# Neighbourhood attention of a two-layer transformer: head pairs scored on the two halves of the rows, position bias added in PSUM, high and low parts of the values side by side in one stationary operand

## The chip, the core and the metric

The kernel runs on one core of a Trainium2 chip. The metric is the device time of one execution in microseconds (us), as the median of several runs. The core has five engines that take their instructions from queues of their own: TensorE (PE in the profile, with its weight loads as PEld), VectorE (DVE), ScalarE (ACT), GpSimd (POOL) and SyncE (SP), which here only issues DMAs.

## The reference

The reference is a two-layer transformer over 256 latent and 256 context tokens, with a width of 1024. Each layer has a feed-forward block, a mixer and another feed-forward block, with adaptive norms between them. The mixer of the second layer is the neighbourhood attention: 16 heads of 64 channels, the 256 latent tokens as a grid of 4 rows by 64 columns, and each query attending to the 16 nearest columns in all 4 rows and to all 256 context tokens.

```
def row_step(args):
    r, q_row = args
    ...
    bias = rpb_cols[:, row_off].transpose(0, 2, 1, 3)
    s_lat = jnp.einsum('bchd,brckhd->bhcrk', q_row, k_nb) * scale + bias
    s_ctx = jnp.einsum('bchd,bkhd->bhck', q_row, k_ctx) * scale
    p = jax.nn.softmax(jnp.concatenate([s_lat.reshape(...), s_ctx], axis=-1), axis=-1)
    ...
    return (jnp.einsum('bhcrk,brckhd->bchd', p_lat, v_nb)
            + jnp.einsum('bhck,bkhd->bchd', p[..., kr * kc:], v_ctx))
```

After it, `y_l = o_l @ w_out` is multiplied by a gate and added to the residual.

## The kernel before

All products run in 32 bits. An operand x is split into a high part of 12 bits and the rest: `split` (L154) takes one ScalarE copy (L156) and one VectorE subtraction (L157). A product of two split operands is then three matmuls, high by high, high by low and low by high (`mm3`, L159 to L162), accumulated in PSUM. So nearly all of the kernel's matmuls stand on lines L160, L161 and L162, and are told apart in the profile by the names of their tiles.

The order of the instructions on each engine is not the order of the text alone: the framework's scheduler lays the operations of independent pieces between each other and sets the queues' order when the kernel is built. On the chip each engine then keeps that order, and waits at an instruction whose inputs are not there. Tiles come from pools of a fixed number of buffers: `pu` has 4 banks of PSUM, `pd` and `ps` have 2 each, `wp` holds 3 raw weight pieces and 4 split ones, `tp` (tiles named by `T`) has 10 buffers, `gp` (`G`) 10.

The neighbourhood attention is `mixer_c` (L931). It works in four steps of four heads (`half`, L940), that is two chunks of 128 channels, each with two heads `m` on partitions 0 to 63 and 64 to 127. A step has these parts:

- The projections of q (256 latent tokens), k and v (512 tokens each), out of weight pieces of 1 MB that SyncE loads (L501) and that are split. q and k come transposed: channels on partitions, tokens along the free axis.
- `scores` (L969), for one head: the position bias is fetched by two DMAs (L982), a mask is added by GpSimd (L983), and the sum is split into `bh` and `bl`. For each of two tiles of 128 queries, three matmuls on the 64 partitions of the head give 512 scores (tiles `k,q`, L991), and two matmuls with the permutation matrix `J` (L992, L993) add the two parts of the bias to the first 256 of them, since the bias comes with its columns reversed. Then VectorE takes the maximum (L662), ScalarE the exponential with its sum (L664), VectorE the reciprocal (L665), and ScalarE scales (L995).
- `values` (L999), for one head: eight transposes of the probabilities (`cst,e`, L672) into two PSUM tiles, each split into `ah` and `al`, and for each of four key tiles the three matmuls of `mm3`: v high by `ah`, v high by `al`, v low by `ah`. The stationary operand is 128 channels wide, that is two heads, and only the 64 rows of the result that belong to the head are read. They are split into `z` (L1007).

The scores of the next head are written ahead of the values of a head (L1014); in the last step three heads are scored ahead. After the fourth step come three parts of the output projection (L1017 to L1019), and then the norm and the last feed-forward block.

The differential attention of the first layer has scores of the same size. There the two halves of a head pair alternate matmul by matmul (L744 to L748):

```
for i in range(3):
    for m in range(2):
        pr = slice(64 * m, 64 * m + 64)
        nc.tensor.matmul(pss[m][:, :n], (qh, qh, ql)[i][pr, qs], (kh, kl, kh)[i][pr, TOK - n :], ...)
```

## Time and profile before

| | |
|---|---|
| median of 3 runs | 1934.93 us (1932.49 to 1937.55) |
| span of the profiled execution, first to last instruction | 1931.2 us |
| PE, PEld busy | 97%, 82% of the span |
| DVE, ACT, POOL busy | 65%, 38%, 4% |
| projections, attention and output projection of the second mixer | from 1490 to 1717 us of the span |

The profile is of one execution. No time of its own besides the span is given for that execution; the span is 3.7 us below the median of the runs. A group's row in the profile gives line, engine and operation, the tiles written and read, the shape, the count, then the busy time in us and the mean duration of one in ns, and behind the second bar the idle time of the engine ahead of these instructions and what ended it. A matmul's duration contains its way through the array, on which the next one already runs; the time that a matmul costs TensorE is the distance from its start to the next start.

### The profile page before, as it was taken

The page shows a single profiled execution, that of the slowest core. Times are in us where ns is not written, and L with a number is a line of the kernel's source. Part 1 is how long each engine was busy: PE and PEld are TensorE (multiplying, and loading weights), DVE is VectorE, ACT ScalarE, POOL GpSimd, SP SyncE. Part 2 cuts the span into 40 slices and gives each one's busy share as a digit, 9 for nine tenths or more (in the row PEclk, how much of TensorE's full clock was granted, in tenths as well). Part 3 has the DMA queues.
Part 4 walks back from the last instruction along what each step waited for, and adds up shares of the span by engine and source line. Part 5 has one row for each costly group of instructions (what it writes and reads, how often), then busy time and mean ns, then how long its engine had stood idle before and what let it go on. Part 6 is the DMA issues. An engine that isn't in the chain of part 4 may idle for free.

```text
span 1931.2 us, 26004 instructions
## 1 busy us (share of the span) xinstructions
PE 1880.6 (97%) x10486; PEld 1586.8 (82%) x10486; DVE 1253.9 (65%) x1948; ACT 740.3 (38%) x1199; POOL 72.3 (4%) x63
## 2 busy tenths in 40 slices
PE   7999999999999999999999999999999999989998
PEld 3878788889877788888888888878889888889998
DVE  5557686666666785976775467763445654576665
ACT  4533233224556234232233242321233555554443
POOL 1000000000100001000000200000000000120000
PEclk9999999999999999999999999999999999989999
DMA  7674555451332322654464224642232333325552
GB/s 260 216 243 171 190 181 196 134 191 30 113 120 77 120 82 80 236 196 153 144 218 161 88 77 163 207 154 84 89 119 84 96 82 80 67 91 193 196 169 73
DMA packets 191153, 271.73 MB, mean 141 GB/s; under 512 B 19703, under 2 KB 139898, under 8 KB 191032
## 3 DMA queue, kind: packets, MB, share of 16 engines
q1 hardware_dynamic: 189468, 267.69, 42.5%
q10 hardware_dynamic: 1260, 2.14, 0.3%
q8 instruction: 82, 1.34, 0.3%
q14 instruction: 39, 0.32, 0.0%
q0 software_dynamic: 304, 0.24, 0.0%
HBM read 262.69 MB, written 7.34 MB: 140 GB/s over the span
## 4 chain that ended last, share of the span: by engine, by line
PE 57%; issue 11%; DVE 3%; DMA 2%; ACT 1%; POOL 1%; SPq 0%; POOLq 0%; DVEq 0%; ACTq 0%
PE pu L160 10%; PE pu L161 10%; PE pu L162 10%; PE pd L160 6%; PE pd L162 6%; PE pd L161 6%; PE ps L160 2%; PE ps L162 2%; PE ps L161 2%; DMA bias<-in_na_rpb_dram 2%; PE ps L672 1%; DVE wl L157 1%; DVE acc L444 1%; PE ps L298 1%; ACT wh L156 0%
## 5 line engine op out<-in xcount | busy, mean ns | idle before, releaser
L162 PE MATMUL pu<-h,wl 128*128 128x512 f32 (+1 forms) x1600 | 544.8, 341 | 3.0 <-POOL wl L157 3.0
L160 PE MATMUL pu<-h,wh 128*128 128x512 f32 (+1 forms) x1600 | 544.4, 342 | 1.8 <-ACT h L488 1.5
L161 PE MATMUL pu<-h,wh 128*128 128x512 f32 (+1 forms) x1600 | 545.4, 341 | 0.1
L156 ACT ACTIVATE wh<-raw 128x1024 fp32r<-128x1024 f32 x228 | 240.6, 1059 | 544.8 <-PE pu L161 417.2
L157 DVE TENSOR_TENSOR wl<-raw,wh 128x1024 fp32r<-128x1024 f32 x216 | 263.0, 1222 | 179.6 <-ACT wh L156 175.3
L160 PEld LDWEIGHTS pu<-h,wh 128*128 128x128 f32 x1600 | 303.1, 190 | 44.5 <-issue 4.2
L162 PEld LDWEIGHTS pu<-h,wl 128*128 128x128 f32 x1600 | 304.0, 190 | 38.5 <-POOL wl L157 3.2
L161 PEld LDWEIGHTS pu<-h,wh 128*128 128x128 f32 x1600 | 304.3, 190 | 34.2 <-DVE h L489 0.7
L287 DVE SCALAR_TENSOR_TENSOR mv<-mw,sF,mv 128x1024 f32<-128x1024 f32 x210 | 258.5, 1279 | 20.9 <-DMA mw<-in_mod_w_dram 20.8
L156 ACT ACTIVATE w<-raw 128x1024 fp32r<-128x1024 f32 x88 | 91.5, 1056 | 163.1 <-PE ps L161 123.4
L552 DVE TENSOR_TENSOR sg<-sg,pu 128x512 f32<-128x512 f32 (+1 forms) x87 | 52.2, 603 | 134.7 <-PE pu L162 127.1
L515 DVE SCALAR_TENSOR_TENSOR res<-pd,gate,res 128x256 f32<-128x256 f32 x244 | 110.9, 478 | 39.8 <-PE pd L162 39.3
L157 DVE TENSOR_TENSOR w<-raw,w 128x1024 fp32r<-128x1024 f32 x88 | 106.9, 1220 | 41.5 <-ACT w L156 41.5
L160 PE MATMUL pd<-g,w 128*128 128x512 f32 (+1 forms) x376 | 133.2, 354 | 0.0
L162 PE MATMUL pd<-g,w 128*128 128x512 f32 (+1 forms) x376 | 132.4, 352 | 0.0
L161 PE MATMUL pd<-g,w 128*128 128x512 f32 (+1 forms) x376 | 132.2, 352 | 0.0
L160 PE MATMUL ps<-g,w 128*128 128x512 f32 (+1 forms) x320 | 116.2, 363 | 0.0
L162 PE MATMUL ps<-g,w 128*128 128x512 f32 (+1 forms) x320 | 116.0, 363 | 0.0
L161 PE MATMUL ps<-g,w 128*128 128x512 f32 (+1 forms) x320 | 116.0, 363 | 0.0
L162 PE MATMUL pd<-h,wl 128*128 128x512 f32 (+1 forms) x288 | 108.2, 376 | 1.6 <-DVE wl L157 1.6
L160 PE MATMUL pd<-h,wh 128*128 128x512 f32 (+1 forms) x288 | 108.6, 377 | 0.0
L161 PE MATMUL pd<-h,wh 128*128 128x512 f32 (+1 forms) x288 | 107.5, 373 | 0.0
(261 smaller groups left out, 2808.6 us busy)
## 6 DMA issues: line engine op xcount, KB each, us to landing
raw<-in_ffn_w_dram SPq DMA_DIRECT2D x132, 1024.0 KB, 5.4
mw<-in_mod_w_dram SPq DMA_DIRECT2D x144, 512.0 KB, 5.9
raw<-in_ab_w_in_dram SPq DMA_DIRECT2D x12, 1024.0 KB, 6.8
raw<-in_na_w_in_dram SPq DMA_DIRECT2D x12, 1024.0 KB
raw<-in_ab_w_out_dram SPq DMA_DIRECT2D x4, 1024.0 KB
raw<-in_na_w_out_dram SPq DMA_DIRECT2D x4, 1024.0 KB
bias<-in_na_rpb_dram SPq DMA_DIRECT2D x32, 96.0 KB, 6.1
dftr<-const_dft_dram SPq DMA_DIRECT2D x5, 256.0 KB
```

The lines of the kernel that those rows point to most:

```text
L156: S.activation(hi, src, AF.Copy)
L157: eng.tensor_tensor(lo, src, hi.bitcast(F32), op=ALU.subtract)
L160: nc.tensor.matmul(ps, wh, xh, start=start, stop=False)
L161: nc.tensor.matmul(ps, wh, xl, start=False, stop=False)
L162: nc.tensor.matmul(ps, wl, xh, start=False, stop=stop)
L287: V.scalar_tensor_tensor(acc, mw, c, acc, op0=ALU.mult, op1=ALU.add)
L298: nc.tensor.matmul(ps[32 * j : 32 * j + 32], row[:, 31 - b : 63 - b], mod_acc[l, i][j % 2][:, j // 2], start=b == 0, stop=b == len(batch) ...
L444: V.tensor_tensor(acc, acc, q, op=ALU.add)
L515: V.scalar_tensor_tensor(res[d][:, sl], ps[:, po], g[:, d, s : s + 1], res[d][:, sl], op0=ALU.mult, op1=ALU.add)
L552: V.tensor_tensor(sg[:, sl], sg[:, sl], p3[:, sl], op=ALU.mult)
L672: nc.tensor.transpose(at[kt // 2][:, o : o + P], e[:, P * kt : P * kt + P], ident)
```

## The change

All of it is in `mixer_c`, and in the constant `J`, which goes.

- The queries are written in reversed columns when they leave PSUM (`turned`). The scores then stand in the order of the fetched bias, and the permutation by `J`, its load and the split of the bias go. VectorE adds the masked bias to the first 256 scores in PSUM.
- `scores` works on two heads. The six matmuls of a query tile alternate between the lower and the upper 64 partitions and write two PSUM tiles. The probabilities of both heads stand in one tile of the pool `gp`.
- The values are stored by head, the 64 high columns beside the 64 low ones. With this stationary operand two matmuls for a key tile, on `ah` and on `al`, give the high products in 64 rows and the low ones in the other 64. ScalarE copies the half of the other rows to the own partitions (`zx`), VectorE adds the two and writes the columns back in their order (`zu`), and the sum is split once for both heads. The product of the low values and `al`, which was left out, is now in the sum.
- The order of the text: per step, scores of the first pair, projection of v, scores of the second pair, values of the first pair, projection of the next q, values of the second pair, projection of the next k. In the last step the first part of the output projection takes the place of the next q.

```diff
-        jt = T(name="jt")[:, :P]
-        nc.sync.dma_start(jt, a["tmp"][:, :P])
-        J = const.tile([P, P], F32R, name="J")
-        S.activation(J, jt, AF.Copy)
...
+        def turned(x):
+            return x.rearrange("p (r c) -> p r c", r=4)[:, :, ::-1]
...
-                S.activation(u, ps[:, :LAT], AF.Copy, scale=0.125)
-                split(*q[i], u)
+                S.activation(turned(u), ps[:, :LAT].rearrange("p (r c) -> p r c", r=4), AF.Copy, scale=0.125)
+                split(*qs[half][i], u)
...
-                split(bh, bl, bias)
...
-                    mm3(ps, q[i][0][pr, qsl], q[i][1][pr, qsl], k[i][0][pr], k[i][1][pr], True, False)
-                    nc.tensor.matmul(ps[:, :256], J, bh[:, e0 : e0 + 256], start=False, stop=False)
-                    nc.tensor.matmul(ps[:, :256], J, bl[:, e0 : e0 + 256], start=False, stop=True)
-                    e, st = softmax_exp(ps, TOK)
-                    S.activation(e, e, AF.Copy, scale=st[:, 2:3])
+                pss = [PU(), PU()]
+                for x, y, n in ((qh, kh, 0), (qh, kl, 1), (ql, kh, 2)):
+                    for m in range(2):
+                        pr = slice(64 * m, 64 * m + 64)
+                        nc.tensor.matmul(pss[m], x[pr, qsl], y[pr], start=n == 0, stop=n == 2)
+                pe = gp.tile([P, 2, TOK], F32, tag="g", name="e")
+                for m in range(2):
+                    ps = pss[m]
+                    V.tensor_tensor(ps[:, :256], ps[:, :256], bias[m][:, e0 : e0 + 256], op=ALU.add)
+                    st = sp.tile([P, 4], F32, tag="sm", bufs=8, name="smx")
+                    V.tensor_reduce(st[:, 0:1], ps, axis=AX.X, op=ALU.max, negate=True)
+                    S.activation(pe[:, m], ps, AF.Exp, bias=st[:, 0:1], accum_out=st[:, 1:2])
+                    V.reciprocal(st[:, 2:3], st[:, 1:2])
+                    S.activation(pe[:, m], pe[:, m], AF.Copy, scale=st[:, 2:3])
...
-                weighted(po, at, 4, lambda kt: [vt[kt // 2][:, kt % 2, x, hs] for x in range(2)])
-                split(zt[pr, i, 0], zt[pr, i, 1], po[pr, :LAT])
+                    w = vt[kt // 2][:, kt % 2, 2 * i + m].rearrange("p a c -> p (a c)")
+                    for n, x in enumerate((ah, al)):
+                        nc.tensor.matmul(po[:, LAT * m : LAT * m + LAT], w, x[:, sl], start=kt == 0 and n == 0, stop=kt == 3 and n == 1)
...
+                S.activation(x[own], po[other, sl], AF.Copy)
+                V.tensor_tensor(turned(u[own]), po[own, sl].rearrange("p (r c) -> p r c", r=4),
+                                x[own].rearrange("p (r c) -> p r c", r=4), op=ALU.add)
+            split(*z[2 * half + i], u)
...
+        for half in range(4):
+            es[half, 0] = scores(half, 0)
+            project_vs(half)
+            es[half, 1] = scores(half, 1)
+            values(half, 0, es[half, 0])
+            if half < 3:
+                project(win, 256 * half + 256, 2, h, project_q(half + 1), PD, [0])
+            else:
+                out_project(wout, range(0, 4), z[0:4], gate, [0])
+            values(half, 1, es[half, 1])
+            if half < 3:
+                project(win, 1024 + 256 * half + 256, 2, h, project_k(half + 1), PD)
```

The change moves instructions on the engines. On TensorE, this is the place before at which the first two heads begin, behind the projection of v (`pd` from `vh,h`): three score matmuls (`k,q`) of one head, then the two of the bias.

```order
L162 MATMUL pd<-vh,h 128x256
L160 MATMUL pu<-k,q 128x512
L161 MATMUL pu<-k,q 128x512
L162 MATMUL pu<-k,q 128x512
L992 MATMUL pu<-bh,J 128x256
L993 MATMUL pu<-bl,J 128x256
L160 MATMUL pu<-k,q 128x512
```

And this is TensorE now at the beginning of the third step, where the projection of k ends and that of v begins; L982 of the changed kernel is the score matmul, L155 to L157 are the three of `mm3`.

```order
L155 MATMUL pd<-h,wh 128x512
L156 MATMUL pd<-h,wh 128x512
L157 MATMUL pd<-h,wl 128x512
L982 MATMUL pu<-k,q 128x512 x12
L155 MATMUL pd<-vh,h 128x256
L156 MATMUL pd<-vl,h 128x256
L157 MATMUL pd<-vh,h 128x256
```

The twelve score matmuls of a pair of heads now stand in one piece, with no bias matmul between them and none behind. Only the very first pair is cut, into two and ten.

On ScalarE, this is the softmax of one head before, in the third step: `e` is the exponential (L664) and its scaling (L995), `ah` the copy of transposed probabilities (L156) of the head ahead of it.

```order
L156 ACTIVATE wh_14026<-raw_14024 128x1024
L156 ACTIVATE z_13249<-pu_13324 64x256
L156 ACTIVATE bh_13348<-bias_13347 128x384
L664 ACTIVATE e_13363,smx_13361<-pu_13355,smx_13361 128x512
L664 ACTIVATE e_13375,smx_13373<-pu_13367,smx_13373 128x512
L995 ACTIVATE e_13363<-e_13363,smx_13361 128x512
L995 ACTIVATE e_13375<-e_13375,smx_13373 128x512
L156 ACTIVATE ah_13390<-ps_13379 128x512
```

And this is ScalarE now in the third step, from the softmax of the second pair (L989, L991) on; the `ah` (L151) belong to the values of the first pair, and `vh` to the weights of the next projection of v.

```order
L989 ACTIVATE e_13237,smx_13239<-pu_13229,smx_13239 128x512
L989 ACTIVATE e_13237,smx_13245<-pu_13230,smx_13245 128x512
L991 ACTIVATE e_13237<-e_13237,smx_13239 128x512
L151 ACTIVATE ah_13282<-ps_13272 128x512
L991 ACTIVATE e_13237<-e_13237,smx_13245 128x512
L989 ACTIVATE e_13258,smx_13260<-pu_13250,smx_13260 128x512
L989 ACTIVATE e_13258,smx_13266<-pu_13251,smx_13266 128x512
L151 ACTIVATE ah_13290<-ps_13273 128x512
L991 ACTIVATE e_13258<-e_13258,smx_13260 128x512
L991 ACTIVATE e_13258<-e_13258,smx_13266 128x512
L151 ACTIVATE ah_13308<-ps_13298 128x512
L151 ACTIVATE vh_13583<-raw_13581 128x1024
```

Two exponentials and a scaling of the second pair now stand ahead of the first `ah` of the first pair, and the rest of that softmax between the next ones. At the same place on TensorE, twelve score matmuls, eight transposes and fourteen matmuls of the next q stand ahead of the first value matmul. On SyncE the eight bias loads of a step now stand in one piece, with three to five weight loads between two such pieces; before they mostly stood in twos and fours between the weight loads. The rest of the program, up to the second mixer and behind it, keeps its order.

More of the change, by code (lines that the diff above doesn't have):

```diff
@@ L51, in constants @@
     cst[:, _CO["ident"]] = np.eye(P)
-    J = np.zeros((P, P))
-    for r2 in range(2):
-        for c in range(64):
-            J[64 * r2 + 63 - c, 64 * r2 + c] = 1.0
-    tmp = np.zeros((P, 384), f32)
-    tmp[:, :P] = J
+    tmp = np.zeros((P, 256), f32)
     cst[:, _CO["sel"]] = np.tile(np.eye(32)[:, :8], (4, 1))
@@ L98 @@
 class _K:
+    pass
 @with_exitstack
@@ L176, in tile_dit @@
     nc.sync.dma_start(w0[:33, :64], a["hy_f_w0"][0])
-    nc.sync.dma_start(w0[:33, 192:448], a["tmp"][:33, P:])
+    nc.sync.dma_start(w0[:33, 192:448], a["tmp"][:33])
     nc.sync.dma_start(w0[:64, 64:192].rearrange("p (i f) -> p i f", i=2), a["hy_f_w1"][0].rearrange("i p f -> p i f"))
@@ new lines, in position, with scores @@
+        def position(hd):
+            b = T(name="bias")[:, :384]
+            b3 = b.rearrange("p (e c) -> p e c", e=6)
+            for r2 in range(2):
+                src = bass.AP(tensor=rpb.tensor, offset=hd * 465 + (5 - r2) * 31 - 48, ap=[[1, 64], [31, 6], [1, 64]])
+                nc.sync.dma_start(b3[64 * r2 : 64 * r2 + 64], src)
+            nc.gpsimd.tensor_tensor(b3, b3, mask, op=ALU.add)
+            return b
+        def scores(half, i):
+            bias = [position(4 * half + 2 * i + m) for m in range(2)]
+            es = []
+            (qh, ql), (kh, kl) = qs[half][i], ks[half][i]
+            for qt in range(2):
+                qsl = slice(P * qt, P * qt + P)
+                e0 = 64 * (2 - 2 * qt)
+                pss = [PU(), PU()]
[12 more added lines that the diff above has]
+                    S.activation(pe[:, m], pe[:, m], AF.Copy, scale=st[:, 2:3])
+                es.append(pe)
+            return es
@@ L1001, in values @@
+        def values(half, i, es):
+            vt = vs[half]
+            po = PU()
+            for m in range(2):
                 at = [PS() for _ in range(2)]
                 for qt in range(2):
-                    transposed(at, es[qt], 4, qt)
-                po = PU()
-                hs = slice(P * i, P * i + P)
-                weighted(po, at, 4, lambda kt: [vt[kt // 2][:, kt % 2, x, hs] for x in range(2)])
-                split(zt[pr, i, 0], zt[pr, i, 1], po[pr, :LAT])
-            heads = [(i, m) for i in range(2) for m in range(2)]
@@ L1010, in mixer_c @@
-            ahead = 1 if half < 3 else 3
-            es = [scores(*hd) for hd in heads[:ahead]]
-            for n, hd in enumerate(heads):
-                if n + ahead < 4:
-                    es.append(scores(*heads[n + ahead]))
-                values(*hd, es[n])
-        gate = gates(1, 5, False)
-        out_project(wout, range(0, 4), z[0:4], gate, [0])
+                    transposed(at, es[qt][:, m], 4, qt)
+                for kt in range(4):
+                    if kt % 2 == 0:
+                        ah, al = T(F32R, name="ah"), T(F32R, name="al")
+                        split(ah, al, at[kt // 2])
+                    sl = slice(256 * (kt % 2), 256 * (kt % 2) + 256)
+                    w = vt[kt // 2][:, kt % 2, 2 * i + m].rearrange("p a c -> p (a c)")
+                    for n, x in enumerate((ah, al)):
+                        nc.tensor.matmul(po[:, LAT * m : LAT * m + LAT], w, x[:, sl], start=kt == 0 and n == 0, stop=kt == 3 and n == 1)
```

70 lines of the change are left out of this document (26 added, 44 removed).

## The prediction

> **What bounds the kernel now.** I first read the page's busy times, then the chain of waits for the pace of the attention's steps, then the busy times of two whole steps.
>
> ```profile
> PE 1880.6 (97%) x10486; PEld 1586.8 (82%) x10486; DVE 1253.9 (65%) x1948; ACT 740.3 (38%) x1199; POOL 72.3 (4%) x63
> ```
>
> ```profile
> 1544.73 1.02 PE ps L672 x8
> ...
> 1594.15 1.02 PE ps L672 x8
> ...
> 1644.72 1.02 PE ps L672 x8
> ```
>
> ```profile
> 1544.73:1594.15 49.42, 47.84 (x313) 41.28 (x314) 25.96 (x46) 27.61 (x56) 3.80 (x5) 1.00 0.35 81
> 1594.15:1644.72 50.57, 49.18 (x313) 42.76 (x314) 25.98 (x46) 27.59 (x56) 3.33 (x4) 0.97 0.33 79
> ```
>
> The same eight transposes return after 49.42 and 50.57 us: one step of four heads takes about 50. The second fence gives, for these two stretches, their length and the busy times of PE, PEld, DVE, ACT and POOL, then the granted clock. In a step PE is busy for 48 to 49 us, DVE for 26, ACT for 27.6. TensorE sets the pace, so a matmul's distance to the next start is worth its full length there, and work on the others is free as long as TensorE does not come to wait for it.
>
> These are the distances, from the order in time on TensorE: six scores of one head and the two matmuls of a projection behind them.
>
> ```profile
> 1524.32 0.50 PE L160 MATMUL pu<-k,q 64*128 64x512 f32 x1
> 1524.66 0.39 PE L161 MATMUL pu<-k,q 64*128 64x512 f32 x1
> 1524.89 0.39 PE L162 MATMUL pu<-k,q 64*128 64x512 f32 x1
> ...
> 1525.90 0.38 PE L160 MATMUL pd<-h,wh 128*128 128x256 f32 x1
> ...
> 1574.35 0.28 PE L161 MATMUL pd<-h,wh 128*128 128x256 f32 x1
> 1574.47 0.28 PE L162 MATMUL pd<-h,wl 128*128 128x256 f32 x1
> ```
>
> A matmul of 512 columns costs 0.23 us, one of 256 columns 0.12. Six scores cost 1.58 us (1524.32 to 1525.90): the first and the step back to 128 rows cost a little more.
>
> **The change part by part.**
>
> *Scores in pairs.* The first layer's attention already alternates the halves, with matmuls of the same shape.
>
> ```profile
> 514.14 1.65 PE L747 MATMUL pu<-qk 64*128 64x512 f32 x12
> 515.73 0.50 PE L160 MATMUL pd<-h,wh 128*128 128x512 f32 x1
> ```
>
> Twelve take 1.59 us there, which twelve at 0.23 could not: the two halves run at the same time. Before, 16 heads cost 16 x 1.58 = 25.3 us; after, 8 pairs cost 8 x 1.59 = 12.7. That is -12.6.
>
> *No `J`.* 16 heads x 4 matmuls of 256 columns, 64 x 0.12 = -7.7 us. Their waits go too:
>
> ```profile
> L992 PE MATMUL pu<-bh,J 128*128 128x256 f32 x24 | 5.9, 323 | 3.0 <-ACT bh L156 3.0
> L992 PE MATMUL pu<-bhl,J 128*128 128x256 f32 x8 | 2.3, 345 | 1.0 <-ACT bhl L156 1.0
> L993 PE MATMUL pu<-bhl,J 128*128 128x256 f32 x8 | 2.0, 306 | 0.2 <-DVE bhl L157 0.2
> ```
>
> TensorE stood idle for 3.0 + 1.0 + 0.2 = 4.2 us ahead of these: -4.2. The bias now has to be there one operation later on VectorE, and its loads stand ahead of the weight loads on SyncE.
>
> ```profile
> L982 SPq DMA_DIRECT2D bias<-in_na_rpb_dram x32: 595/614/646, 1467.1 to 1677.4; - x32
> ...
> DMA to landing us min/median/max: 5.9/6.1/7.4
> ```
>
> The loads of a step, eight of 6 us each and 0.6 us of issue, are asked for when the buffers of the values are free; that is in the values of a step's pairs, some 10 us ahead of the next scores (the last 37 projection matmuls of k alone are 37 x 0.23 = 8.5 us). I take the bias at nothing; if that cover fails, each step waits some us at its first addition. The three weight loads queued behind these are wanted half a step later.
>
> *Values.* 16 heads x 4 key tiles x one matmul of 256 columns less: 64 x 0.12 = -7.7 us.
>
> *Scores no longer laid between values.* Before, six times (two heads in each of the first three steps) the scores of one head were cut up among the values of another, as in this stretch and the next:
>
> ```profile
> 1540.74 0.31 PE L160 MATMUL pu<-ah,v 128*128 128x256 f32 x1
> 1540.98 0.49 PE L160 MATMUL pu<-k,q 64*128 64x512 f32 x1
> ...
> 1544.66 1.09 PE L672 MATMUL ps<-cst,e 128*128 128x128 f32 x8
> 1545.51 0.47 PE L160 MATMUL pd<-h,wh 128*128 128x512 f32 x1
> ```
>
> ```profile
> 1553.08 0.38 PE L160 MATMUL pu<-ah,v 128*128 128x256 f32 x1
> ...
> 1556.78 0.49 PE L672 MATMUL ps<-cst,e 128*128 128x128 f32 x3
> ```
>
> They take 3.92 and 3.70 us, where six scores in one piece and twelve values are 1.58 + 12 x 0.12 = 3.02: each change between 64 and 128 rows costs about 0.1 us. Three of each are 3 x 0.90 + 3 x 0.68 = 4.7; now the values lie only between matmuls of 128 rows: -4.7.
>
> So TensorE is relieved by 12.6 + 7.7 + 4.2 + 7.7 + 4.7 = 36.9 us, 9.2 for each step.
>
> *The new chain of the softmax.* The bias addition in PSUM has no row before. It lies between nothing (the maximum had to read PSUM anyway) and a whole 512-column pass (0.69); nearest is a VectorE operation of its size out of PSUM.
>
> ```profile
> L157 DVE TENSOR_TENSOR v<-pd,v 128x256 fp32r<-128x256 f32 x16 | 6.7, 418 | 3.0 <-ACT v L156 3.0
> L662 DVE TENSOR_REDUCE smx<-pu 128x1 f32<-128x512 f32 x32 | 20.7, 686 | 19.1 <-PE pu L993 18.8
> L156 ACT ACTIVATE ah<-ps 128x512 fp32r<-128x512 f32 x32 | 18.5, 597 | 0.6 <-PE ps L672 0.6
> L157 DVE TENSOR_TENSOR bl<-bias,bh 128x384 fp32r<-128x384 f32 x11 | 6.1, 556 | 9.5 <-ACT bh L156 9.1
> ```
>
> I take 0.42. For a step VectorE then loses 4 splits of `bl` (0.56) and 4 of z (0.42) and gains 8 additions, 4 `zu` and 2 z (0.42 each): 26.0 - 3.9 + 5.9 = 28 us. ScalarE loses 4 `bh` and gains about one operation: below 27. The reversed writes of `u` and `zu` have no row either; even at twice the time they are 24 operations, 10 us of VectorE and ScalarE over the mixer, off the chain except for the very last z, which has some 25 matmuls of the output projection (3 us) ahead of its use. By their sums, neither engine limits a step of 50 - 9.2 = 41 us. Their order does.
>
> The place is the first value matmul of each step. It waits for `ah`, and on ScalarE two exponentials and a scaling of the second pair stand ahead of that.
>
> ```profile
> 1577.96 0.69 ACT L664 ACTIVATE e<-pu,smx 128x512 f32<-128x512 f32 x1 [1.80 <-DVE smx L662]
> ...
> 1578.64 0.68 ACT L664 ACTIVATE e<-pu,smx 128x512 f32<-128x512 f32 x1
> ...
> 1579.30 1.33 ACT L995 ACTIVATE e<-e,smx 128x512 f32<-128x512 f32 x2
> 1580.53 0.38 ACT L948 ACTIVATE u<-pd 128x256 f32<-128x256 f32 x1
> ```
>
> An exponential takes 0.67, a scaling 0.62. From the start of the second pair's scores: its first two tiles are done after half of 1.59 and the rest of a matmul, about 0.95; two additions and a maximum, 2.48; two exponentials, 3.82; a scaling, 4.44; `ah`, 5.04. TensorE has 1.59 of scores, eight transposes (1544.66 to 1545.51, 0.85) and 14 x 0.12 = 1.68 ahead: 4.12. So it waits 0.9 us. The next `ah` and `al` of the pair stand behind the rest of that softmax and the splits of two weights; followed in the same way they come between 0.0 and 0.2 late, five or six times. I take 2.0 us for a step, +8. The ends are 0 (an `ah` with nothing ahead of it on ScalarE would be done at 1.59 + 0.85 + 0.60 = 3.04, before TensorE asks for it) and 4.5 (five such waits, all as long as the first).
>
> *The clock.* In the second stretch above the clock was 0.97, in the first 1.00, and both held one wait of this size:
>
> ```profile
> 1576.21 0.51 PE L992 MATMUL pu<-bh,J 128*128 128x256 f32 x2 [1.34 <-ACT bh L156]
> ...
> 1625.45 0.79 PE L992 MATMUL pu<-bh,J 128*128 128x256 f32 x2 [1.15 <-ACT bh L156]
> ```
>
> One wait of about 1.2 us in two brought 50.57 x 0.03 = 1.5 us of loss. Before there was one such loss among the steps, and I leave one. The Trainium skill (TensorE: Matmul & The Clock Gate, Part 1: The HAM clock gate) has the clock halved only after an idle window of about 3.4 us; by that the new waits would cost no clock at all and my sum would stand, while by the row it could be 1.5 us for each step more. The row speaks against the rule, so the upper end carries it.
>
> *Sum.* -36.9 + 8 = -28.9 us. The span is 1931.2, so 1902.3; what lies around it doesn't change, and from the median of the runs, 1934.93, it is 1906.0 us.
>
> **The rivals.**
>
> *The pairs gain and the evacuation takes it back.* Each pair hands VectorE and ScalarE four tiles at once, and both queues serve them ahead of the next `ah`. For it speaks the 0.9 us above; against it the busy sums, 28 and 27 of 41 us. If the whole gain of the pairing (12.6) is waited for again, it gives 1906 + 12.6 = 1919, and with a clock loss in each step 1925. The Trainium skill (TensorEngine Tiling (Array Packing), Performance Considerations) has the rule: packing speeds up TensorE but not the emptying of PSUM, which may become the bottleneck. 12 in 100.
>
> *The pairs do not run side by side here.* Then the scores cost 96 x 0.23 + 8 x 0.2 = 23.7 instead of 12.7, and it comes to 1917. Against it stands the same form at 514.14. 3 in 100.
>
> *Slower: ScalarE's queue holds the values up.* Between the third and the fourth `ah` stands a copy of the next v weights, which waits for a DMA; were that, or the bias ahead of it on SyncE, late in each step, all values behind would wait. It decides from 9.2 us a step on, where the relief is used up. At 10 us a step and a clock loss each, 4 x 11.5 - 36.9 = +9: 1944. Against it: those loads are asked for most of a step ahead, and the bias needs only 6 to 7 us. 5 in 100.
>
> **How the numbers follow.** The forecast, with new waits of 0 to 4.5 us a step, has 80 in 100: from 1934.93 - 36.9 = 1898 to 1898 + 18 = 1916, and 1896 if the one clock loss goes as well. The rivals have 12, 3 and 5. The range that holds 8 in 10 runs from 1896 to 1921: it takes in the forecast's own range and the first rival up to its middle. A measurement here can tell about 0.3% (5.8 us) from no change. Slower by that needs over 10.7 us of new waits a step: 5 in 100. Within it, 7.8 to 10.7 us a step: 5 in 100. Faster: 90.
>
> **What would show it right or wrong.** Twelve scores from one block to the next in 1.6 us; no idle time at an addition of the bias; a distance between two steps' transposes of 42 to 43 us; idle time of TensorE at the first value matmul of a step of about 1 us and not more than 2 a step in all. It is wrong if steps take 46 us or more, or if the waits stand at bias additions, or if DVE or ACT is busy for over 90% of a step.

## The result and the profile after

| | before | after |
|---|---|---|
| median of the runs on one chip | 1936.24 us (1932.49 to 1938.17) | 1903.98 us (1901.99 to 1906.16) |
| span of the profiled execution | 1931.2 us | 1900.3 us |
| PE, DVE, ACT busy in the span | 1880.6, 1253.9, 740.3 us | 1850.6, 1257.0, 738.0 us |

The ratio is 0.983 (0.982 to 0.985): 32 us less. The prediction said 1906.0 and 1896 to 1921. Its time lies 2 us from the median; its gain, 28.9 us, is 3.4 smaller than the measured 32.3, and not every term of its sum held.

Line numbers are now those of the changed kernel: the matmuls of `mm3` are L155 to L157, `split` L151 and L152, the scores L982, the bias addition L986, the exponential L989, the scaling L991, the transposes L667, the values L1012. The first fence has the busy times of two whole steps, from the first pair's scores to the first pair's scores of the next step (length, then PE, PEld, DVE, ACT, POOL, then the granted clock).

```profile
1552.59:1594.79 42.20, 40.54 (x281) 35.77 (x281) 26.80 (x52) 26.56 (x55) 4.09 (x5) 1.00 0.36 94
1594.79:1636.82 42.03, 41.06 (x282) 35.85 (x282) 26.70 (x52) 26.55 (x55) 4.25 (x5) 1.00 0.35 95
```

A step takes 42.1 us where it took 49.42 and 50.57. For the whole mixer, these are the stretches from its first matmul to the first matmul of the next block, before and after:

```profile
1490.53:1728.18 237.65, 224.19 (x1513) 197.96 (x1513) 140.75 (x262) 132.49 (x267) 25.08 (x21) 0.98 0.33 84
```

```profile
1491.15:1695.61 204.46, 193.09 (x1386) 173.41 (x1384) 141.36 (x285) 128.47 (x258) 23.84 (x18) 0.98 0.33 93
```

The mixer is 33.2 us shorter and the rest of the span 2.3 longer. TensorE's busy time in the mixer fell by 31.1 us, its idle time from 13.5 to 11.4: nearly all of the gain is work that TensorE no longer does. TensorE still sets the pace, and VectorE and ScalarE are busy for 64% of a step. The order in time on TensorE around the second pair of a step (the last bracket of a row is the idle time ahead of it and what ended it):

```profile
1565.89 1.65 PE L982 MATMUL pu<-k,q 64*128 64x512 f32 x12
1567.47 1.09 PE L667 MATMUL ps<-cst,e 128*128 128x128 f32 x8
1569.51 0.39 PE L155 MATMUL pd<-h,wh 128*128 128x256 f32 x1 [0.95 <-ACT e L989]
...
1579.59 0.38 PE L1012 MATMUL pu<-ah,v 128*128 128x256 f32 x1 [0.28 <-ACT ah L151]
1580.41 0.50 PE L155 MATMUL pd<-h,wh 128*128 128x512 f32 x1 [0.43 <-ACT u L943]
```

Twelve scores take 1.58 us from block to block, as in the first layer. Five of the eight pairs run in such a block; the very first is cut into two and ten, and the second pairs of the last two steps take 2.27 and 2.29 us, held up in the middle by a wait for `v`. Over the whole mixer these groups of TensorE wait (behind the second bar: the idle time and its releasers), and VectorE's additions of the bias stand below them:

```profile
L155 PE MATMUL pd<-h,wh 128*128 128x256 f32 (+1 forms) x96 | 33.1, 345 | 1.9 <-ACT e L989 0.9 <-ACT u L943 0.9
L1012 PE MATMUL pu<-ah,v 128*128 128x256 f32 x64 | 19.8, 313 | 1.0 <-ACT ah L151 1.0
L1012 PE MATMUL pu<-al,v 128*128 128x256 f32 x64 | 17.7, 299 | 1.1 <-DVE al L152 1.1
L982 PE MATMUL pu<-k,q 64*128 64x512 f32 x96 | 14.3, 415 | 0.6 <-DVE v L152 0.6
L155 PE MATMUL pd<-vh,h 128*128 128x256 f32 x128 | 36.8, 288 | 0.6 <-DVE v L152 0.6
L155 PE MATMUL pd<-z,wh 128*128 128x256 f32 x64 | 19.0, 297 | 3.0 <-DVE res L510 3.0
L986 DVE TENSOR_TENSOR pu<-pu,bias 128x256 f32<-128x256 f32 x32 | 12.5, 422 | 1.2 <-PE pu L982 1.1
```

The first five add up to 5.2 us of waits in the steps, 1.3 a step. The additions take 0.422 us each and wait for their scores, never for the bias.

### The profile page after: what moved, and what is told of

Read it like the earlier page. It is cut to its first block, busy times and chain, and to the rows that moved or that the text cites. A ratio compares the mean times of both kernels' runs of the same rounds, so it can differ in the third digit from the quotient of the medians.

```text
span 1900.3 us, 25792 instructions
## 1 busy us (share of the span) xinstructions
PE 1850.6 (97%) x10358; PEld 1566.0 (82%) x10358; DVE 1257.0 (66%) x1972; ACT 738.0 (39%) x1190; POOL 73.6 (4%) x63
## 4 chain that ended last, share of the span: by engine, by line
PE 67%; DVE 4%; ACT 2%; issue 1%; POOL 1%; DMA 0%; SPq 0%; DVEq 0%; ACTq 0%
PE pu L155 11%; PE pu L156 11%; PE pu L157 11%; PE pd L155 7%; PE pd L157 7%; PE pd L156 7%; PE ps L155 3%; PE ps L156 3%; PE ps L157 3%; PE pu L1012 1%; DVE wl L152 1%; PE ps L667 1%; DVE acc L439 1%; PE pu L982 1%; PE ps L293 1%
## 5 line engine op out<-in xcount | busy, mean ns | idle before, releaser
L157 PE MATMUL pu<-h,wl 128*128 128x512 f32 (+1 forms) x1600 | 545.6, 342 | 3.0 <-POOL wl L152 3.0
L155 PE MATMUL pu<-h,wh 128*128 128x512 f32 (+1 forms) x1600 | 545.0, 342 | 1.6 <-ACT h L483 1.5
L156 PE MATMUL pu<-h,wh 128*128 128x512 f32 (+1 forms) x1600 | 546.0, 342 | 0.1
L151 ACT ACTIVATE wh<-raw 128x1024 fp32r<-128x1024 f32 x228 | 240.3, 1058 | 558.6 <-PE pu L156 403.2
L152 DVE TENSOR_TENSOR wl<-raw,wh 128x1024 fp32r<-128x1024 f32 x216 | 263.7, 1225 | 203.8 <-ACT wh L151 177.6
L155 PEld LDWEIGHTS pu<-h,wh 128*128 128x128 f32 x1600 | 303.8, 191 | 44.1 <-issue 4.2
L157 PEld LDWEIGHTS pu<-h,wl 128*128 128x128 f32 x1600 | 304.7, 191 | 38.4 <-POOL wl L152 3.3
L156 PEld LDWEIGHTS pu<-h,wh 128*128 128x128 f32 x1600 | 304.9, 191 | 33.8 <-DVE h L484 0.5
L151 ACT ACTIVATE w<-raw 128x1024 fp32r<-128x1024 f32 x88 | 91.5, 1057 | 164.2 <-PE ps L156 120.5
L152 DVE TENSOR_TENSOR w<-raw,w 128x1024 fp32r<-128x1024 f32 x88 | 107.0, 1221 | 42.0 <-ACT w L151 41.9
L155 PE MATMUL pd<-g,w 128*128 128x512 f32 (+1 forms) x376 | 133.6, 355 | 0.0
L157 PE MATMUL pd<-g,w 128*128 128x512 f32 (+1 forms) x376 | 132.6, 353 | 0.0
L156 PE MATMUL pd<-g,w 128*128 128x512 f32 (+1 forms) x376 | 132.6, 353 | 0.0
L155 PE MATMUL ps<-g,w 128*128 128x512 f32 (+1 forms) x320 | 116.3, 363 | 0.0
L157 PE MATMUL ps<-g,w 128*128 128x512 f32 (+1 forms) x320 | 116.1, 363 | 0.0
L156 PE MATMUL ps<-g,w 128*128 128x512 f32 (+1 forms) x320 | 116.1, 363 | 0.0
L155 PE MATMUL pd<-h,wh 128*128 128x512 f32 (+1 forms) x288 | 108.3, 376 | 1.9 <-ACT e L989 0.9
L157 PE MATMUL pd<-h,wl 128*128 128x512 f32 (+1 forms) x288 | 107.6, 374 | 1.7 <-DVE wl L152 1.7
L156 PE MATMUL pd<-h,wh 128*128 128x512 f32 (+1 forms) x288 | 106.9, 371 | 0.0
```

Of the source, the lines that this page charges most:

```text
L151: S.activation(hi, src, AF.Copy)
L152: eng.tensor_tensor(lo, src, hi.bitcast(F32), op=ALU.subtract)
L155: nc.tensor.matmul(ps, wh, xh, start=start, stop=False)
L156: nc.tensor.matmul(ps, wh, xl, start=False, stop=False)
L157: nc.tensor.matmul(ps, wl, xh, start=False, stop=stop)
```

## The experiments

All times are medians of several runs beside runs of the kernel before on the same chip; the ratio to those is given with its interval. Code is shown against the changed kernel.

**The changed kernel a second time.**

> The changed kernel once more, on the same chip as the next three, as what they are measured against. Both theories: 1904 us, that is 32 us below the kernel before (ratio 0.983).

Measured: 1904.4 us, ratio 0.984 (0.982 to 0.985). Its steps repeat those of the first profile (the next one takes 42.04 us):

```profile
1555.31:1597.51 42.20, 40.54 (x281) 35.75 (x280) 26.80 (x52) 26.57 (x55) 3.69 (x4) 1.00 0.37 94
```

So a step's length tells kernels apart to about 0.1 us, while medians of the whole differ by 0.4 us and spans of the same kernel by 2.7 (1900.3 and 1903.0). The experiments are read by their steps first.

**Heads in turn.** The six matmuls of a query tile in the order of the heads, three and three.

```diff
-                for x, y, n in ((qh, kh, 0), (qh, kl, 1), (ql, kh, 2)):
-                    for m in range(2):
+                for m in range(2):
+                    for x, y, n in ((qh, kh, 0), (qh, kl, 1), (ql, kh, 2)):
```

> The same twelve score matmuls of a pair, but the three of the lower half first and then the three of the upper, so that neighbours use the same rows of the array. Theory (TensorE's own time sets the steps): twelve take 2.8 to 3.0 us instead of 1.6, 8 x 1.2 to 1.4 = 10 to 11 us slower than the changed kernel, 1914 to 1915. Rival (the gain is the new order of the projections, and what the pairing saves is waited for again behind the softmax): the first head's scores are there as early as before, TensorE waits less at the values, and the time stays within 2 us of 1904.

Measured: 1903.0 us, ratio 0.983 (0.981 to 0.985). The theory fell, and with it the idea that this edit undoes the pairing; the time that the rival gave was met, but not for the rival's reason. The queue was built as written, three of one PSUM tile and then three of the other:

```
L982 MATMUL pu_12581<-k_12507,q_12377 128x512 x3
L982 MATMUL pu_12582<-k_12507,q_12377 128x512 x3
L982 MATMUL pu_12602<-k_12507,q_12377 128x512 x3
L982 MATMUL pu_12603<-k_12507,q_12377 128x512 x3
```

and yet the trace's order in time has the block last 1.59 us:

```profile
1552.02 1.66 PE L982 MATMUL pu<-k,q 64*128 64x512 f32 x12
1553.61 0.39 PE L155 MATMUL pd<-vh,h 128*128 128x256 f32 x1
```

The halves ran side by side although the queue does not alternate: a matmul on the other half starts while earlier ones of the first half are still waiting. The edit also moved the second pair's scores ahead in the built order, and its steps are shorter than those of the change:

```profile
1552.02:1593.17 41.15, 40.56 (x281) 35.80 (x281) 27.44 (x52) 26.55 (x55) 3.23 (x4) 1.00 0.39 96
1593.17:1634.59 41.42, 40.57 (x281) 35.82 (x281) 27.75 (x52) 26.56 (x55) 4.45 (x4) 1.00 0.36 97
```

**Six and six.** All six matmuls of the lower half (both query tiles), then all six of the upper.

```diff
-            for qt in range(2):
...
+            for m in range(2):
+                pss = [PU(), PU()]
+                for qt in range(2):
...
+                    for x, y, n in ((qh, kh, 0), (qh, kl, 1), (ql, kh, 2)):
+                        nc.tensor.matmul(pss[qt], x[pr, qsl], y[pr], start=n == 0, stop=n == 2)
```

> Both heads of a pair are scored, but first all six matmuls of the lower half (both query tiles), then all six of the upper half. In the run with three and three in turn the halves still ran side by side: the trace has the third matmul of either head start within 0.01 us of each other. Theory: TensorE only looks a few matmuls ahead for work on the other half, so six in a row are too many; the twelve then take 12 x 0.23 + 0.2 = 2.96 us in place of 1.58, 8 x 1.38 = 11 us more for TensorE, of which the waits give back up to two thirds as they did when the third value matmul was put back: 1908 to 1915. Rival: it looks ahead far enough, the twelve take 1.6 us and the time stays from 1901 to 1906.

Measured: 1906.65 us, ratio 0.985 (0.983 to 0.986). The block's length lies between those of the theory and the rival:

```profile
1556.07 2.22 PE L982 MATMUL pu<-k,q 64*128 64x512 f32 x12
1558.22 0.38 PE L155 MATMUL pd<-vh,h 128*128 128x256 f32 x1
```

The block takes 2.15 us, neither 1.58 nor the 2.96 of twelve in a row. That is 0.57 or two and a half slots of 0.23 more than side by side. By the start times of the single matmuls, the first of the upper half begins together with the third of the lower (1556.64), when two are through and four still to do. So the reach here is about four matmuls.

**Apart, and the control side by side.** To keep the halves apart, a matmul of 32 columns over all 128 rows (zeros, overwritten by the scores) stands ahead of each head; the control has the same matmuls ahead of both heads and alternates.

```diff
+        zero = const.tile([P, 32], F32R, name="zero")
+        S.activation(zero, ident[:, :32], AF.Copy, scale=0.0)
...
-                for x, y, n in ((qh, kh, 0), (qh, kl, 1), (ql, kh, 2)):
-                    for m in range(2):
+                for m in range(2):
+                    nc.tensor.matmul(pss[m][:32, :32], zero, zero, start=True, stop=True)
+                    for x, y, n in ((qh, kh, 0), (qh, kl, 1), (ql, kh, 2)):
```

> The two heads of a pair are scored in turn, three matmuls and three, and ahead of each three stands a matmul of 32 columns over all 128 rows (zeros, into the PSUM tile that is overwritten next), so that the halves cannot run side by side: in 12 of the 16 query tiles, since in four the extra matmuls were built far ahead of the scores. The extra matmuls are priced by the run with the same ones ahead of both heads. Theory of the prediction: the pairing is worth its matmuls; a tile apart costs 6 x 0.23 and two more steps to and from 128 rows where side by side it is 3 x 0.23 and one, so 0.95 us more, 12 tiles 11.4 us, of which the waits give back no more than they did for the values (a third): 7 to 12 us above the run side by side, 1912 to 1919. Rival (what the pairs gain is waited for again): within 3 us of the run side by side.

> The changed kernel with the same 32 extra matmuls of 32 columns over 128 rows, both ahead of the alternating six of a query tile, so that the halves still run side by side. It prices what the extra matmuls cost by themselves: 32 at about 0.05 and 16 steps to and from 128 rows at 0.2, 4 to 5 us at most, part of it in waits that are there anyway: 1904 to 1909.

Measured: apart 1920.54 us, ratio 0.992 (0.991 to 0.993); side by side 1906.15 us, ratio 0.985 (0.983 to 0.986). The difference is 14.4 us. Apart:

```profile
1525.32 0.18 PE L983 MATMUL pu<-zero 128*32 128x32 f32 x1
1525.43 0.94 PE L986 MATMUL pu<-k,q 64*128 64x512 f32 x3
1526.30 0.20 PE L983 MATMUL pu<-zero 128*32 128x32 f32 x1
1526.43 0.96 PE L986 MATMUL pu<-k,q 64*128 64x512 f32 x3
```

and side by side:

```profile
1551.45 0.21 PE L983 MATMUL pu<-zero 128*32 128x32 f32 x2
1551.59 0.98 PE L987 MATMUL pu<-k,q 64*128 64x512 f32 x6
1552.50 0.23 PE L983 MATMUL pu<-zero 128*32 128x32 f32 x2
```

One head alone takes 1.0 us (1525.43 to 1526.43), two side by side 1.05 (1551.45 to 1552.50): a tile apart costs 0.95 us more. By the start times 14 of the 16 tiles were apart, two more than expected, so the work is 13.3 us. But the difference is not that work alone. In the profiled executions the mixer, up to the first matmul of the next block, takes 221.3 us apart and 205.9 side by side, 15.4 more. With the heads apart TensorE's clock is at 0.50 twice among the scores, from 1528.97 and from 1607.47, for 3.41 us each; the control has no such loss there, and it makes up 3.4 of the 15.4. And in whole steps a part of the work goes into idle time. Here is a step with three tiles apart, and a step of the control:

```profile
1559.90:1603.85 43.95, 43.95 (x288) 37.52 (x287) 27.36 (x52) 27.09 (x55) 4.31 (x4) 1.00 0.35 90
```

```profile
1551.59:1594.22 42.63, 41.56 (x291) 36.18 (x288) 26.83 (x52) 26.52 (x55) 5.58 (x6) 1.00 0.37 95
```

TensorE is busy for 2.4 us more, its 1.1 us of idle time are gone, and the step is 1.3 longer. So without the clock the pairing is worth some 12 us here: most of its work, as the theory has it, though the difference of the medians lies above the theory's 7 to 12. The rival that the pairs' gain is waited for again, with 3 us at most, has fallen. The scheduler laid out the two queues differently in other places too, so 12 is not exact.

**Values with three matmuls.** The low values in a stationary operand of their own, as before.

```diff
-                    w = vt[kt // 2][:, kt % 2, 2 * i + m].rearrange("p a c -> p (a c)")
-                    for n, x in enumerate((ah, al)):
-                        nc.tensor.matmul(po[:, LAT * m : LAT * m + LAT], w, x[:, sl], ...)
+                    vh, vl = [vt[kt // 2][:, kt % 2, y, P * i : P * i + P] for y in range(2)]
+                    mm3(po[:, LAT * m : LAT * m + LAT], vh, vl, ah[:, sl], al[:, sl], kt == 0, kt == 3)
...
-                S.activation(x[own], po[other, sl], AF.Copy)
-                V.tensor_tensor(turned(u[own]), ...)
+                S.activation(turned(u[own]), po[own, sl].rearrange("p (r c) -> p r c", r=4), AF.Copy)
```

> Values as in the kernel before: the high and the low parts in two stationary operands of 128 channels, three matmuls for a key tile, and no copy of the other half (the low values times al are left out again). The rest as in the changed kernel. Theory: 64 more matmuls of 256 columns, 64 x 0.12 = +7.7 us, 1911 to 1912. Rival (they go into the waits for ah and al that TensorE has there): less than half of it, 1904 to 1907.

Measured: 1906.86 us, ratio 0.985 (0.984 to 0.987). Two steps:

```profile
1552.73:1595.77 43.04, 42.58 (x297) 37.54 (x296) 25.07 (x48) 26.47 (x55) 2.16 (x3) 1.00 0.33 90
1595.77:1638.74 42.97, 42.56 (x297) 37.52 (x297) 25.50 (x48) 26.47 (x55) 3.69 (x5) 1.00 0.34 93
```

TensorE has 1.8 us more to do in a step (42.57 and 40.80, the means), but the step is only 0.9 longer (43.0 and 42.1): its idle time falls from 1.3 us to 0.4. The 16 matmuls of a step cost what they should, and half of that was standing idle anyway. (The edit also takes VectorE's addition of the halves off the way to `z`, which may have shortened a wait.) The groups say the same: of the waits for `ah`, `al`, `e` and `u`, 4.0 us in the changed kernel, 0.8 are left.

```profile
L155 PE MATMUL pd<-h,wh 128*128 128x256 f32 (+1 forms) x96 | 33.0, 344 | 0.2
L155 PE MATMUL pu<-ah,v 128*128 128x256 f32 x64 | 19.7, 308 | 0.5 <-ACT ah L151 0.3
L156 PE MATMUL pu<-al,v 128*128 128x256 f32 x64 | 19.0, 297 | 0.1
```

**The bias by `J` again.** The bias is split and added by the two matmuls with the permutation, here behind the six scores of a query tile; the halves still alternate, and the reversed writes go.

```diff
-                        nc.tensor.matmul(pss[m], x[pr, qsl], y[pr], start=n == 0, stop=n == 2)
+                        nc.tensor.matmul(pss[m], x[pr, qsl], y[pr], start=n == 0, stop=False)
+                for m in range(2):
+                    for n in range(2):
+                        nc.tensor.matmul(pss[m][:, :256], J, bias[m][n][:, e0 : e0 + 256], start=False, stop=n == 1)
...
-                    V.tensor_tensor(ps[:, :256], ps[:, :256], bias[m][:, e0 : e0 + 256], op=ALU.add)
```

> The bias is split and added by two matmuls with the permutation J again, behind the twelve scores of a pair; queries and results keep their column order, and VectorE's addition in PSUM goes. Theory: 64 matmuls of 256 columns, +7.7 us, and some tenths for each change from 64 to 128 rows, no waits for the bias since it is loaded early: 1912 to 1914. Rival (the waits for the bias were what counted, 4.2 us before, and J itself is cheap where TensorE waits anyway): 1904 to 1908, or with the waits back, over 1916.

Measured: 1917.26 us, ratio 0.990 (0.989 to 0.992), 13 us above the change. Steps take 45.35 us, 3.2 more, and 4 x 3.2 = 12.9:

```profile
1561.31:1606.66 45.35, 44.34 (x298) 37.93 (x297) 26.28 (x48) 28.77 (x59) 3.48 (x4) 1.00 0.35 88
```

The waits that the rival and the prediction's 4.2 us stand for did not come back: TensorE is idle for 1.0 us in this step. It is busy for 3.5 us more than in the change, 14 in four steps, where the 64 matmuls of 0.12 are 7.7. What comes on top fits the queue: the matmuls with `J` now stand between the scores, so that a pair's twelve come as six, four and two (1606.66, 1607.99 and 1608.97) with changes between 64 and 128 rows.

**The old order of the text.** The three projections of a step first, then the scores and values of both pairs.

```diff
+            if half:
+                project(win, 256 * half, 2, h, project_q(half), PD, [0])
+                project(win, 1024 + 256 * half, 2, h, project_k(half), PD)
+            project_vs(half)
             es[half, 0] = scores(half, 0)
-            project_vs(half)
             es[half, 1] = scores(half, 1)
             values(half, 0, es[half, 0])
-            if half < 3:
-                project(win, 256 * half + 256, 2, h, project_q(half + 1), PD, [0])
-            else:
-                out_project(wout, range(0, 4), z[0:4], gate, [0])
             values(half, 1, es[half, 1])
-            if half < 3:
-                project(win, 1024 + 256 * half + 256, 2, h, project_k(half + 1), PD)
+        out_project(wout, range(0, 4), z[0:4], gate, [0])
```

> Text order of before in the changed kernel: the q, k and v projections of a step, then the scores and values of both pairs, the output projection at the end. In the built order the second pair's scores follow the first's after some ten matmuls of a projection, and the values of both pairs stand together with nothing but their transposes between. Theory: the order of the text is a part of the gain, since the projections between scores and values are what hides the softmax; each pair is then waited for by 2 to 4 us: 8 x 2 to 4 less the 5.2 of waits that go = 11 to 27 us more: 1915 to 1931. Rival: the scheduler lays enough of the next step's projection between, and the order of the text is worth less than 5 us: up to 1909.

Measured: 1923.91 us, ratio 0.994 (0.992 to 0.995): 20 us of the 32 are gone. Steps take 45.9:

```profile
1572.37:1618.30 45.93, 42.30 (x282) 36.69 (x281) 26.79 (x53) 26.80 (x54) 4.19 (x4) 1.00 0.32 87
```

TensorE is busy for 42.30 us, 1.5 more than in the change, and idle for 3.6 instead of 1.3. The order on TensorE shows where:

```profile
1572.37 1.65 PE L982 MATMUL pu<-k,q 64*128 64x512 f32 x12
1575.10 0.97 PE L982 MATMUL pu<-k,q 64*128 64x512 f32 x6
1577.10 0.66 PE L667 MATMUL ps<-cst,e 128*128 128x128 f32 x4 [1.03 <-ACT e L991]
1577.92 0.96 PE L982 MATMUL pu<-k,q 64*128 64x512 f32 x3
1579.52 0.60 PE L667 MATMUL ps<-cst,e 128*128 128x128 f32 x4
1580.29 0.96 PE L982 MATMUL pu<-k,q 64*128 64x512 f32 x3
```

Scores and transposes of both pairs now meet: the last tile of the second pair is cut into three and three with matmuls of 128 rows between, so it isn't side by side any more, and the transposes wait for a softmax with nothing to cover it. In the first step a clock loss of 1.7 us comes on top (it is shown with the clock below).

**No scaling, no maximum.** Two kernels that each relieve one engine and leave a part of the softmax out: the first the division by the sum (ScalarE), the second the maximum, with a quarter of the scores in the exponential (VectorE).

```diff
-                    S.activation(pe[:, m], pe[:, m], AF.Copy, scale=st[:, 2:3])
```

```diff
-                    V.tensor_reduce(st[:, 0:1], ps, axis=AX.X, op=ALU.max, negate=True)
-                    S.activation(pe[:, m], ps, AF.Exp, bias=st[:, 0:1], accum_out=st[:, 1:2])
+                    S.activation(pe[:, m], ps, AF.Exp, scale=0.25, accum_out=st[:, 1:2])
```

> The division of the probabilities by their sum is left out, so ScalarE loses 32 scalings of 0.62 us, four of them in the queue ahead of each ah that a pair waits for. Theory of the prediction: the waits for ah, al, e and u that came with the pairs (5.2 us in the four steps) are ScalarE's queue, so they nearly go, 4 to 5 us less: 1899 to 1900. Rival: they come from VectorE or from TensorE's own order (too few matmuls between scores and transposes); then less than 1.5 us goes: 1902.5 to 1905.

> Leaves out the maximum over the scores (and takes the exponential of a quarter of them), so VectorE loses 32 passes of 0.68 us and the first exponential of a pair no longer waits for two additions and two maxima. Without ScalarE's scalings the steps stayed at 42.0 us. Theory: what TensorE waits for in a step (5.2 us in all four: e, ah, al, u) is the start of the softmax on VectorE, where both heads' additions and then both maxima lie ahead of the first exponential, 2.7 us behind the pair's first score; without the maxima it starts 1.3 us earlier, steps come to 41.0 to 41.5 us and the time to 1899 to 1902. Rival: the waits move to other places (PSUM banks that ScalarE empties late), steps stay at 41.8 to 42.2 and the time at 1902.5 to 1905.

Measured: 1906.18 us, ratio 0.985 (0.983 to 0.986), and 1905.96 us, ratio 0.985 (0.984 to 0.986). Steps without the scaling, then without the maximum:

```profile
1551.83:1593.88 42.05, 40.38 (x282) 35.58 (x282) 27.25 (x52) 21.72 (x47) 5.41 (x5) 1.00 0.38 96
```

```profile
1553.56:1595.98 42.42, 40.96 (x281) 35.76 (x280) 22.04 (x44) 26.02 (x55) 5.07 (x6) 1.00 0.37 95
```

ScalarE has 4.8 us less to do in a step, and the step takes 42.05; VectorE has 4.8 less, and it takes 42.4. Both theories fell, and the times lie 1 us above the rivals' ranges too: relief of one engine alone doesn't shorten a step. That neither engine causes the waits in the change isn't shown by it, because the scheduler laid the queues anew and TensorE stands at other places: without the scaling it waits 2.4 us for `ah` in two steps, where it was 0.6.

**The next weights by VectorE.** While the mixer ends, GpSimd works out four low parts of the next block's weights; here VectorE does it.

```diff
-        ws = ws or ffn_first(l, j, nc.gpsimd)
+        ws = ws or ffn_first(l, j, V if (l, j) == (1, 1) else nc.gpsimd)
```

> The four low parts of the first weights of the last feed-forward block, which GpSimd works out (2.4 us each) while the mixer ends, are worked out by VectorE. Theory: VectorE's additions acc, 2.2 to 2.6 us at that place in place of 0.42, are slow because GpSimd works beside them on the same memory; they fall to about 0.42, the residual is no longer late and the wait of 3.0 us at the last output projection goes: 1901 to 1902. Rival: the additions are slow for another reason, or the four subtractions of 1.2 us now stand ahead of the residual in VectorE's queue: 1904 to 1908.

Measured: 1901.68 us, ratio 0.982 (0.981 to 0.984), at the theory's place but with an interval that overlaps that of the change. Half of its mechanism is seen in the order in time on VectorE and GpSimd, in the changed kernel:

```profile
1684.79 2.09 DVE L439 TENSOR_TENSOR acc<-acc,sq 128x256 f32<-128x256 f32 x1 [0.15 <-ACT sq L437]
```

```profile
1684.23 2.37 POOL L152 TENSOR_TENSOR wl<-raw,wh 128x1024 fp32r<-128x1024 f32 x1 [1.61 <-ACT wh L151]
```

and with the weights on VectorE:

```profile
1688.15 0.96 DVE L439 TENSOR_TENSOR acc<-acc,sq 128x256 f32<-128x256 f32 x2 [0.15 <-ACT sq L437]
```

An addition that begins during GpSimd's operation takes 2.09 us and ends 0.3 behind it (1686.88 and 1686.60); without GpSimd two take 0.96. The other half isn't: the waits for `res` at the last output projection, 3.0 us in the change, come to 2.5 here, and the theory had them gone.

**Both that were a little faster.** Heads in turn and the weights on VectorE.

> Two edits that each took nothing or little, together: heads scored three and three in turn (steps of 41.2 to 41.4 us there, but more waits in the output projection at the end), and the first weights of the last feed-forward block split by VectorE. If the waits at the end are the slow additions on VectorE, the shorter steps now show: 1899 to 1901. If they are TensorE's own order there, nothing is gained over the second edit alone: 1901 to 1904.

Measured: 1902.17 us, ratio 0.983 (0.981 to 0.984): nothing over the second edit alone. The shorter steps of heads in turn (41.2 us here too) do not reach the end, so the slow additions were not what swallowed them, or not alone. No version beats the change by more than the measurements can tell.

## Why the prediction was right, and where it was not

*The bound and the size.* TensorE does set the pace: steps were forecast at 42 to 43 us and take 42.1. The sum had TensorE's work fall by 12.6 + 7.7 + 7.7 + 4.7 = 32.7 us and its waits grow by 8 - 4.2 = 3.8. In the mixer the busy time fell by 31.1, and the idle time fell by 2.1 instead of growing. So the work was forecast well, the waits with the wrong sign, and that the rest of the span is 2.3 us longer hides a part of it: the closeness of the time to 2 us is partly luck.

*The pairs.* Side by side as in the first layer, 1.58 us for twelve, and worth most of their price: held apart, a tile costs 0.95 us of TensorE, and 14 tiles some 12 us besides the clock losses, where the sum had 12.6 for all 16. The rival "evacuation takes it back" (12 in 100) is refuted by the two runs with the extra matmul; VectorE and ScalarE are busy for 27 of 42 us. The rule of the Trainium skill that stood beside it (TensorEngine Tiling (Array Packing), Performance Considerations) speaks of a TensorE made four times as fast; with two halves, this kernel doesn't reach that limit. The rival with pairs that don't run together fell with the 1.58 us, and the slower one with waits of 1.3 us a step where it needed 9.2. The prediction took alternation to be what makes the halves run together. It isn't needed: three and three in turn did as well.

*No `J`.* 11.9 predicted, as 7.7 of matmuls and 4.2 of waits; 12.9 measured in company of the pairs. That the two agree is luck: with `J` back, the waits did not return, and the rest above 7.7 is TensorE's busy time, as the scores are cut up again. The addition cost 0.42 and never waited for a bias, as forecast.

*The values.* Here the sum is wrong in form. The term of -7.7 is right in TensorE's work (1.8 us a step) and half as large in time (0.9 a step; 2.5 in the medians of the two kernels on the same chip), because TensorE is idle for 1.3 us a step in the change and only for 0.4 with the third matmul in place. Relief and new waits were put down as two terms; here they are one.

*The new waits.* 2.0 us a step forecast, 1.3 found, so 5.2 instead of 8: with that, 36.9 - 5.2 = 31.7, where the medians have 32.3. But the place was wrong by half: the value matmuls wait 2.1 us in all, and the first of a step, forecast to wait 0.9, doesn't wait in any of the four (the row with 0.28 above is a later one). In the last three steps it starts 5.2 to 5.4 us behind the pair's first score, not far from the forecast's 5.04, but TensorE has lost the time ahead of it: 0.95 at a projection's first matmul, released by an exponential, in one step, and among the scores themselves in the other two. The cause given, ScalarE's queue with two exponentials and a scaling ahead of `ah`, is not borne out: without the scalings the steps are as long as before, though in another order of the queues.

*The order of the text.* The prediction gave it -4.7, for scores no longer cut up among values. Undone by itself it costs 20 us: it also keeps the pairs whole and lays projections over the softmax. That the new waits stay at 1.3 us a step is its doing, which the sum took for granted. The prices found by undoing one part at a time (14 with its clock losses, 13, 3 and 20) add up to more than 32, so none of them is a share of the gain.

*The clock.* One loss among the steps was left in the sum, and there is none after, which is worth 1.7 us (3.4 us at half the clock). The loss before had been put down to a wait of 1.2 us. These windows show more: the stretch ahead of the loss and the loss, before; the stretch of the wait of 0.95 and the next, after; and, in the run with the heads apart, a stretch and the next in the last scores of its first step, with a block of twelve in its fourth step below them; and, in the run with the projections first, the end of its first step.

```profile
1622.30:1625.45 3.15, 1.99 (x10) 1.38 (x10) 0.02 (x1) 0.52 (x1) 0.86 (x1) 1.00 0.85 238
1625.45:1628.80 3.35, 3.35 (x15) 3.35 (x16) 1.96 (x4) 0.94 (x3) 0.00 (x0) 0.50 0.59 151
```

```profile
1565.89:1569.51 3.62, 2.67 (x21) 1.90 (x20) 3.54 (x8) 2.16 (x5) 0.00 (x0) 1.00 0.01 2
1569.51:1573.00 3.49, 3.49 (x28) 3.45 (x29) 3.46 (x8) 3.49 (x9) 0.00 (x0) 1.00 0.00 0
```

```profile
1525.43:1529.00 3.57, 3.57 (x16) 2.23 (x15) 2.56 (x7) 1.89 (x6) 0.00 (x0) 1.00 0.75 261
1529.00:1532.40 3.40, 3.40 (x15) 2.75 (x15) 2.25 (x6) 1.10 (x3) 0.00 (x0) 0.50 0.00 0
...
1650.29:1654.25 3.96, 3.96 (x17) 2.23 (x15) 2.90 (x5) 1.47 (x3) 2.22 (x2) 1.00 0.17 21
```

```profile
1534.80:1538.20 3.40, 1.79 (x13) 1.39 (x12) 0.73 (x3) 3.40 (x8) 0.00 (x0) 1.00 0.15 49
1538.20:1541.62 3.42, 3.08 (x14) 3.08 (x15) 2.49 (x4) 2.52 (x5) 0.00 (x0) 0.50 0.00 0
```

With the heads apart TensorE was busy for all of 3.57 us, but for four short matmuls on 64 of its 128 rows, and lost half its clock for the next 3.4. The same happened at 1607.47, behind twelve more scores apart, and did not happen in the third block of this kind, at 1650.29. So a wait isn't needed for the loss, and matmuls on half the rows over about 3.5 us can come before it but don't always. Nor are they needed: with the projections first, all matmuls ahead of the loss are on 128 rows, and TensorE was idle for nearly half of the stretch. Before, 64-row scores and a wait of 1.15 us shared such a stretch. After, a similar wait beside scores on both halves cost nothing. That the clock goes by the rows in use over a stretch, idle time counted as none, would fit the four losses; it is argued from these places, not shown. The two losses with the heads apart begin 78.50 us apart, 23 times 3.413; if TensorE's work is weighed in stretches of that length counted from them, the blocks at 1525.43 and 1603.85 fill one whole and the block at 1650.29 none, which would be why it was spared. The Trainium skill (TensorE: Matmul & The Clock Gate, Part 1: The HAM clock gate) speaks of idle windows of about 3.4 us; the length of the losses agrees, 3.4 us here, but none of these stretches was idle as a whole, and that with the heads apart not at all.

*What stays open.* What sets the last 1.3 us of waits in a step. Relief on ScalarE or on VectorE comes with other queues, in which the waits stand elsewhere and are no shorter; two other built orders (three and three, six and six) have steps of 41.2 to 41.6 us and give it back in the output projection and behind it. No run here takes work away and holds the order fixed, so each price above contains what the new order did.

## What to carry to other kernels

When one engine sets the pace, count relief and new waits as one term: here half of what the third value matmul took off it came back as idle time. Put work that needs nothing between a score and its use and keep 64-row matmuls of both halves together; here that order was worth more than any single saving, and undoing it took 20 of 32 us. When a difference between two runs is priced, look at the clock and the idle time of both first: of the 15.4 us that the mixer took longer with the heads apart, 3.4 were clock. Before an edit is used to undo a part, look in the trace whether it did: writing the heads in turn undid nothing.

## What the runs showed of the hardware

- Matmuls on the two halves of the rows run side by side without alternating in the queue, with a reach of about four in this order: 1.59 us for twelve in threes, 2.15 in sixes, and 1.0 us for three of 512 columns with a 128-row matmul between heads.
- TensorE's clock fell to 0.50 for 3.4 us behind 3.57 us of uninterrupted matmuls, all but four short ones on 64 rows; it did so in two of three such blocks of one run.
- An addition on VectorE with both inputs in SBUF, of which two take 0.96 us alone, took 2.09 beside a GpSimd operation of 2.37 and ended 0.3 us behind it. The Trainium skill (SBUF — State Buffer, Who interferes with whom) has a VectorE instruction with two SBUF inputs contend with a GpSimd instruction that reads SBUF, over a port pair that the two share as an exclusive lock, which these rows agree with.
